# SSD decays from running sums that are spread over the partitions by DMA, in a two-layer Mamba-2 and stick-breaking trunk

## The chip, the cores and the metric

The kernel runs on one core of a Trainium2 chip. The core has TensorE (PE, matmuls; its weight loads are listed as PEld), VectorE (DVE), ScalarE (ACT), GpSimd (POOL) and SyncE (SP, which here only issues DMAs). They run side by side, each one through its own list of instructions in order, and wait for each other on semaphores. The metric is the device time of one execution in microseconds, as the median of several runs.

## The reference, cut to what matters

The input is one sequence of 512 tokens of width 1024. Layer 0 is a Mamba-2 (SSD) mixer with a squared-ReLU MLP behind it, layer 1 a stick-breaking attention with a second MLP; each of the four is followed by a LayerNorm on the scaled residual. Only the mixer's scan is touched. With 32 heads in 8 groups, a state of 128 and a time step for each head and token:

```python
dt = softplus(dt_raw + dt_bias)
a  = -exp(a_log)
da = dt * a                                   # log decay of one token, one head
a_cs = cumsum(da) within a chunk              # running sums
decay_mat = exp(segsum(da))                   # exp(a_cs[t] - a_cs[s]) for s <= t, otherwise 0
y_diag = einsum("bcgls,bcgrls,bcsgrp->bclgrp", C B^T, decay_mat, x * dt)
states = B^T (exp(a_cs[-1] - a_cs) * x * dt)  # carried from chunk to chunk
y_off  = C state * exp(a_cs)
y = rms_norm((y_diag + y_off + d * x) * silu(z)) @ w_out
```

The reference uses chunks of 64 tokens; the kernel uses chunks of 128, which gives the same sums.

## The kernel before, in words

All large products keep float32 precision by splitting both factors into a high part, rounded to the format that TensorE reads (float32r), and a low part, the rest. `mm3` (lines 206 to 209) then makes three matmuls: high by high, high by low, low by high. Weights come by DMA on SP's queue through two raw buffers; ScalarE casts the high part (line 190), and VectorE subtracts the low part (line 192), GpSimd for every fourth weight.

The mixer works on 8 groups of 4 heads, and on 4 chunks of 128 tokens, a tile having 128 partitions. For each group, `in_bc` and `in_x` project the input onto B, C and two tiles of x, `conv` applies the causal convolution and SiLU, `in_xt` turns x so that tokens lie on partitions and multiplies it by the time step, and `in_z` projects the gate. `time_steps` makes the time steps of all heads once, at the start: a projection, a transposition, softplus by elementwise work on VectorE, the log decays `da` (split into `da_h` and `da_l`), and four small matmuls with a triangle of ones and with all ones, which give the running sums and the chunks' totals. Their exponentials are `E`, `bdec` and `dec_s`.

`decays` then makes for a group and each chunk the matrix exp(a_cs[t] - a_cs[s]), with s on the partitions and, in one row, four heads by 128 tokens t. GpSimd writes `da[s]` where t >= s and 0 elsewhere (line 771, once for the high and once for the low part, into `dm`); two matmuls with a triangle (lines 774 and 775) sum it over the partitions into PSUM; ScalarE takes the exponential (line 777). `scores` makes B against C for all chunks, copies it to SBUF and lets GpSimd zero the part above the diagonal (line 788). `front` multiplies decays by scores (line 799, on GpSimd for chunk 3 and on VectorE for the others), splits the product into the factor `W` (lines 801 and 802) and updates the state. `back` multiplies `W` with x and the carried state with C. `gate` and `finish` apply the gate and the group's norm and transpose the result.

The order is a planner's, with a simulated clock: it takes the program order as priority, and issues on each engine what it thinks is ready. Program order is: the group's own `front` and `back` steps, and between them, as fillers, steps of projections of the next group and of this group's gate. After groups 3 and 7 the output projection follows. `table_order` keeps SiLU and exponential instructions of ScalarE from mixing, since they need different tables.

Of the kernel before, what the change touches and what calls it, by code (L numbers as in the profile page):

```python
# [35 lines left out]
def trunk(ctx: ExitStack, tc: tile.TileContext, io):  # L36
# [5 lines left out]
    lp = ctx.enter_context(tc.tile_pool(name="lp", bufs=2))  # L42
    ps = ctx.enter_context(tc.tile_pool(name="ps", bufs=4, space=PSUM))

    def psum(tag, shape, name):
        return ps.tile(shape, F32, tag=tag, name=name, bufs=4)
# [20 lines left out]
    for _ in range(14):  # L67
# [497 lines left out]
    def ssm(sp, nxt_ln):  # L565
# [48 lines left out]
        bdec = small("bdec")  # L614
        dec_s = small("dec_s")

        def time_steps():
            w = wdt
            pd = psum("mm", [P, T], "pdt")
            proj(pd, w, x_)  # L620
            dT = sp.tile([P, T], F32, tag="cacc", name="dT", bufs=3)
# [23 lines left out]
            nc.vector.tensor_copy(da_h, da)  # L645
            nc.vector.tensor_sub(da_l, da, f(da_h))
            pa = psum("bg", CH, "pacs")
            pt_ = psum("bg", CH, "ptot")
            for o, l in ((pa, tri_le), (pt_, ones_r)):
                nc.tensor.matmul(o, l, da_h, start=True, stop=False)  # L650
                nc.tensor.matmul(o, l, da_l, start=False, stop=True)
            nc.scalar.activation(E, pa, AF.Exp)
            nc.scalar.activation(bdec, pt_, AF.Exp)
# [107 lines left out]

        def decays(q, cs=range(NT)):
            g = q.g
            hs = slice(4 * g, 4 * g + 4)
            if cs[0] == 0:
                q.dec = []
            for c in cs:
                nm = f"{g}_{c}"
                dm = pair(f"dm{nm}", S4, "dm", 1)
                for o, i in zip(dm, (da_h, da_l)):  # L770
                    nc.gpsimd.affine_select(o, f(i[:, c, hs]).unsqueeze(2).to_broadcast(S4), pattern=[[0, 4], [1, P]],
                                            compare_op=ALU.is_ge, fill=0.0, base=0, channel_multiplier=-1)
                pseg = psum("bg", S4, f"sg{nm}")
                nc.tensor.matmul(pseg, tri_gt, dm[0], start=True, stop=False)
                nc.tensor.matmul(pseg, tri_gt, dm[1], start=False, stop=True)
                dec = sp.tile(S4, F32, tag="dec", name=f"dec{nm}", bufs=4)
                table_order("exp", nc.scalar.activation(dec, pseg, AF.Exp))
                q.dec.append(dec)

        def scores(q):  # L780
            g = q.g
            pcb = psum("bg", [P, NT, P], f"cb{g}")
            for c in range(NT):
                cs = slice(c * P, (c + 1) * P)
                mm3(pcb[:, c, :], (q.B[0][:, cs], q.B[1][:, cs]), (q.C[0][:, cs], q.C[1][:, cs]), True, True)
            q.cbm = sp.tile([P, NT, P], F32, tag="cbm", name=f"cbm{g}", bufs=1)
            nc.scalar.copy(q.cbm, pcb)
            nc.gpsimd.affine_select(q.cbm, q.cbm, pattern=[[0, NT], [1, P]], compare_op=ALU.is_ge, fill=0.0,
                                    base=0, channel_multiplier=-1)
            q.pr = [None] * NT  # L790
            q.W = [None] * NT

        def front(q, c):
# [3 lines left out]
            dec = q.dec[c]  # L797
            eng = nc.gpsimd if c == 3 else nc.vector
            eng.tensor_tensor(dec, dec, q.cbm[:, c, :].unsqueeze(1).to_broadcast(S4), op=ALU.mult)
            W = q.W[c] = pair(f"W{nm}", S4, "W", 2)  # L800
# [74 lines left out]

        cur = Group(0)
        time_steps()
        run(in_bc(cur, 0))
        run(in_bc(cur, 1))
        run(in_x(cur, 0))  # L880
        run(in_x(cur, 1))
        decays(cur)
        in_xt(cur)
        v = None
        for g in range(G):
# [15 lines left out]
            front(q, 1)  # L901
            fill.run(5)
            back(q, 0)
            fill.run(4)
            front(q, 2)
            fill.run(4)
            back(q, 1)
            fill.run(4)
            front(q, 3)
            fill.run(4)  # L910
# [21 lines left out]
            if g % 4 == 3:  # L932
# [5 lines left out]
                else:  # L938
                    nxt_ln.load_rows(lambda j, c0: sp.tile(S4, F32, tag="dec", name=f"lnr{j}{c0}", bufs=4)
                                     .rearrange("p a c -> p (a c)"), T)  # L940
# [339 lines left out]
```

## Time and profile before

| | before |
|---|---|
| median of 3 runs | 1426.51 us (1426.31 to 1427.24) |
| the profiled execution's own time | 1426.79 us |
| its span, from first to last instruction | 1424.7 us |
| mean granted TensorE clock | 0.994 |
| TensorE busy | 1394.1 us, 98% |
| VectorE, ScalarE, GpSimd busy | 1078.2, 783.9, 221.4 us |
| the mixer | the first 430 us, roughly |

A profile page lists, for each engine, its busy time; a group of instructions has its line in the kernel, its engine and operation, output and inputs by name, its shape, the count, the busy time, the mean duration in ns, and the idle time of the engine just before it with what ended that. In a timeline the first two numbers are the start and the duration in us. [...]

### The profile page before, as it was taken

Reading aid. Unit: us, or ns where it says so; the run is one execution under the profiler, and the core shown is the slowest. Engines: PE = TensorE matmul, PEld = TensorE weight load, DVE = VectorE, ACT = ScalarE, POOL = GpSimd, SP = SyncE. Lnnn points to the kernel's source line nnn. Section 1 sums busy time; section 2 is a strip of 40 time slices with the busy share of each in tenths; the row PEclk is TensorE's granted clock in tenths of the full one; section 3 lists DMA queues with packets and bytes.
Section 4 is the critical chain, followed back from the end, with each engine's and each line's share of the span. In section 5 each row is a group of like instructions: output and inputs, shape, how many; then the busy total and the mean of one; then the engine's idle time right before and its main releaser. Section 6 shows DMA issues by size and latency. Waiting matters only on the chain. (4 is left out here: it accounts for less than half of the span.)

```text
span 1424.7 us, 19323 instructions
## 1 busy us (share of the span) xinstructions
PE 1394.1 (98%) x7414; PEld 1199.9 (84%) x7414; DVE 1078.2 (76%) x1530; ACT 783.9 (55%) x1264; POOL 221.4 (16%) x249
## 2 busy tenths in 40 slices
PE   9999999999999999999999899999999999999996
PEld 6898897889997988888888789899878888888885
DVE  5798898368877695876849868787867876858587
ACT  5556574246653453626345468898842735454453
POOL 2344555135443100000000200000000000000001
PEclk9999999999999999999999999999999999999999
DMA  5223212221223356455443421121223455454533
GB/s 185 75 77 131 75 60 75 89 89 60 75 75 104 125 157 179 132 179 161 148 148 120 146 89 38 52 75 45 89 75 118 131 165 162 149 175 136 176 111 126
DMA packets 46699, 162.99 MB, mean 114 GB/s; under 512 B 5520, under 2 KB 5776, under 8 KB 46608
## 3 DMA queue, kind: packets, MB, share of 16 engines
q1 hardware_dynamic: 44016, 157.44, 35.4%
q10 hardware_dynamic: 2592, 4.33, 1.0%
q8 instruction: 58, 0.95, 0.3%
q14 instruction: 33, 0.27, 0.1%
HBM read 159.65 MB, written 2.10 MB: 114 GB/s over the span
## 5 line engine op out<-in xcount | busy, mean ns | idle before, releaser
L190 ACT CAST wh<-wr 128x1024 fp32r<-128x1024 f32 x235 | 246.7, 1050 | 328.5 <-DMA wr<-w 165.1
L192 DVE TENSOR_TENSOR wl<-wr,wh 128x1024 fp32r<-128x1024 f32 x218 | 268.4, 1232 | 184.3 <-ACT wh L190 182.9
L208 PE MATMUL f<-ln_hl,wh 128*128 128x512 f32 (+1 forms) x544 | 201.2, 371 | 0.0
L209 PE MATMUL f<-ln_hh,wl 128*128 128x512 f32 (+1 forms) x544 | 201.1, 370 | 0.0
L207 PE MATMUL f<-ln_hh,wh 128*128 128x512 f32 (+1 forms) x544 | 200.4, 371 | 0.0
L208 PEld LDWEIGHTS f<-ln_hl,wh 128*128 128x128 f32 x544 | 102.3, 188 | 17.6 <-DVE ln_hl L399 0.2
L209 PEld LDWEIGHTS f<-ln_hh,wl 128*128 128x128 f32 x544 | 102.3, 188 | 17.4
L207 PEld LDWEIGHTS f<-ln_hh,wh 128*128 128x128 f32 x544 | 101.9, 188 | 17.5
L347 POOL TENSOR_TENSOR ln_rs<-ln_sums 128x1 f32<-128x1 f32 (+1 forms) x6 | 3.1, 523 | 635.3 <-ACT lnr L345 635.3
L208 PE MATMUL X<-wl,hP 128*128 128x512 f32 x192 | 74.7, 389 | 0.0
L207 PE MATMUL X<-wh,hP 128*128 128x512 f32 x192 | 74.7, 389 | 0.0
L209 PE MATMUL X<-wh,l 128*128 128x512 f32 x192 | 74.2, 390 | 0.2 <-DVE l L460 0.2
L209 PE MATMUL pz<-wh,x_l 128*128 128x256 f32 x256 | 72.8, 284 | 0.0
L208 PE MATMUL pz<-wl,x_h 128*128 128x256 f32 x256 | 72.6, 284 | 0.0
L207 PE MATMUL pz<-wh,x_h 128*128 128x256 f32 x256 | 72.5, 283 | 0.0
L459 ACT CAST hP<-r 128x512 fp32r<-128x512 f32 x80 | 48.1, 620 | 32.4 <-DVE r L471 31.5
L192 POOL TENSOR_TENSOR wl<-wr,wh 128x1024 fp32r<-128x1024 f32 x17 | 42.5, 2503 | 93.3 <-ACT wh L190 92.9
L207 PE MATMUL px<-x_h,wh 128*128 128x512 f32 x128 | 50.8, 397 | 0.0
L208 PE MATMUL px<-x_l,wh 128*128 128x512 f32 x128 | 50.2, 393 | 0.0
L209 PE MATMUL px<-x_h,wl 128*128 128x512 f32 x128 | 50.2, 392 | 0.0
L208 PE MATMUL Y<-wl,hP 128*128 128x512 f32 x128 | 49.8, 389 | 0.0
L208 PEld LDWEIGHTS pz<-wl,x_h 128*128 128x128 f32 x256 | 48.7, 190 | 0.9
(1365 smaller groups left out, 3930.7 us busy)
## 6 DMA issues: line engine op xcount, KB each, us to landing
wr<-w SPq DMA_DIRECT2D x160, 512.0 KB, 3.6
wr<-w_bc SPq DMA_DIRECT2D x16, 512.0 KB, 3.6
wr<-w_x SPq DMA_DIRECT2D x16, 512.0 KB, 3.6
wr<-w_z SPq DMA_DIRECT2D x16, 512.0 KB, 3.5
wr<-w_so SPq DMA_DIRECT2D x16, 512.0 KB, 3.6
rawa<-w SPq DMA_DIRECT2D x16, 512.0 KB, 3.6
rawc<-w SPq DMA_DIRECT2D x16, 512.0 KB, 4.5
wr<-w_qk SPq DMA_DIRECT2D x16, 512.0 KB, 3.6
```

Source lines behind the costliest of these rows:

```text
L190: nc.scalar.copy(hi, raw)
L192: eng.tensor_sub(lo, raw, f(hi))
L207: nc.tensor.matmul(out, a[0], b[0], start=start, stop=False, skip_group_check=skip)
L208: nc.tensor.matmul(out, a[0], b[1], start=False, stop=False, skip_group_check=skip)
L209: return nc.tensor.matmul(out, a[1], b[0], start=False, stop=stop, skip_group_check=skip)
L347: nc.gpsimd.tensor_add(rs, self.sq[:, t0:t1, 0], self.sq[:, t0:t1, 1])
L459: nc.scalar.copy(h, src)
```

## The change

Four things change in the mixer.

First, the decays. One exponential of a difference is written as exp(a_cs[t] + (-a_cs[s])). `time_steps` keeps the negated running sums `ncs` with tokens on partitions, and makes the running sums a second time, laid out as rows (chunk and head on partitions, tokens along the row) by two more matmuls; a copy and a DMA put these rows into a DRAM tensor `cs_rows`. The new `spread` reads, for a group and a chunk, the four heads' rows of 128 tokens back by a DMA that repeats them on all 128 partitions, and GpSimd replaces what lies above the diagonal by -1e30 in place. `decays` then is four exponentials of 128 columns for each chunk, one for each head, in place and with `ncs` as a bias for each partition. The selects into `dm`, the two matmuls and the constant `tri_gt` go. The `dec` tiles come from 6 buffers instead of 4; the `dm` tiles' memory is free.

Second, the scores are no longer masked, since the decay is already exactly 0 above the diagonal, and `front` multiplies chunk 3 on VectorE like the others.

Third, the order. At the start, the steps of the time steps' projection alternate in program order with B's, and from the fifth on with two of C's each; the rest of `time_steps` is cut in two by a `yield`, of which the second part stands between the two x projections. `spread` for the next group follows each `front`.

Fourth, after group 3 `decays` for the next group comes behind `finish` instead of ahead of it.

```diff
+    dp = ctx.enter_context(tc.tile_pool(name="dp", bufs=1, space=bass.MemoryType.DRAM))
...
-    tri_gt = cp.tile([P, P], F32R, name="tri_gt")
-    nc.gpsimd.affine_select(tri_gt, one, pattern=[[-1, P]], compare_op=ALU.is_gt, fill=0.0,
-                            base=0, channel_multiplier=1)
...
+        ncs = small("ncs")
+        cs_rows = dp.tile([NT, H, P], F32, name="cs_rows")
...
-        def time_steps():
-            w = wdt
-            pd = psum("mm", [P, T], "pdt")
-            proj(pd, w, x_)
+        def time_steps(pd):
...
+            yield
             pa = psum("bg", CH, "pacs")
             pt_ = psum("bg", CH, "ptot")
...
+            pr = psum("mm", [P, P], "pcsr")
+            for i, x in enumerate((da_h, da_l)):
+                nc.tensor.matmul(pr, x.rearrange("p c h -> p (c h)"), tri_le, start=i == 0, stop=i == 1)
+            rows = sp.tile([P, P], F32, name="csr")
+            nc.scalar.copy(rows, pr)
+            nc.sync.dma_start(cs_rows.rearrange("c h t -> (c h) t"), rows)
+            nc.scalar.activation(ncs, pa, AF.Copy, scale=-1.0)
...
-        def decays(q, cs=range(NT)):
...
-                dm = pair(f"dm{nm}", S4, "dm", 1)
-                for o, i in zip(dm, (da_h, da_l)):
-                    nc.gpsimd.affine_select(o, f(i[:, c, hs]).unsqueeze(2).to_broadcast(S4), pattern=[[0, 4], [1, P]],
-                                            compare_op=ALU.is_ge, fill=0.0, base=0, channel_multiplier=-1)
-                pseg = psum("bg", S4, f"sg{nm}")
-                nc.tensor.matmul(pseg, tri_gt, dm[0], start=True, stop=False)
-                nc.tensor.matmul(pseg, tri_gt, dm[1], start=False, stop=True)
-                dec = sp.tile(S4, F32, tag="dec", name=f"dec{nm}", bufs=4)
-                table_order("exp", nc.scalar.activation(dec, pseg, AF.Exp))
+        def spread(q, c):
+            g = q.g
+            if c == 0:
+                q.dec = []
+            dec = sp.tile(S4, F32, tag="dec", name=f"dec{g}_{c}", bufs=6)
+            nc.sync.dma_start(dec.rearrange("p h t -> p (h t)"),
+                              cs_rows[c, 4 * g:4 * g + 4, :].rearrange("h t -> (h t)").partition_broadcast(P))
+            nc.gpsimd.affine_select(dec, dec, pattern=[[0, 4], [1, P]], compare_op=ALU.is_ge, fill=-1e30,
+                                    base=0, channel_multiplier=-1)
+            q.dec.append(dec)
+
+        def decays(q):
+            for c, dec in enumerate(q.dec):
+                for h in range(4):
+                    i = 4 * q.g + h
+                    table_order("exp", nc.scalar.activation(dec[:, h, :], dec[:, h, :], AF.Exp,
+                                                            bias=ncs[:, c, i:i + 1]))
...
-            nc.gpsimd.affine_select(q.cbm, q.cbm, pattern=[[0, NT], [1, P]], compare_op=ALU.is_ge, fill=0.0,
-                                    base=0, channel_multiplier=-1)
...
-            eng = nc.gpsimd if c == 3 else nc.vector
-            eng.tensor_tensor(dec, dec, q.cbm[:, c, :].unsqueeze(1).to_broadcast(S4), op=ALU.mult)
+            nc.vector.tensor_tensor(dec, dec, q.cbm[:, c, :].unsqueeze(1).to_broadcast(S4), op=ALU.mult)
...
-        time_steps()
-        run(in_bc(cur, 0))
-        run(in_bc(cur, 1))
+        pd = psum("mm", [P, T], "pdt")
+        b_steps, c_steps = in_bc(cur, 0), in_bc(cur, 1)
+        for k, _ in enumerate(proj_steps(pd, wdt, x_)):
+            next(b_steps)
+            if k >= KD // 2:
+                next(c_steps)
+                next(c_steps)
+        steps = time_steps(pd)
+        next(steps)
+        run(b_steps)
+        run(c_steps)
         run(in_x(cur, 0))
+        run(steps)
         run(in_x(cur, 1))
+        for c in range(NT):
+            spread(cur, c)
         decays(cur)
...
+            def first(c):
+                front(q, c)
+                if nxt:
+                    spread(nxt, c)
+
             scores(q)
             fill.run(4)
-            front(q, 0)
+            first(0)
...
-            if nxt:
+            if nxt and g % 4 < 3:
                 decays(nxt)
             finish(q, 1 if nxt else 2)
+            if nxt and g % 4 == 3:
+                decays(nxt)
```

More of the change, by code (lines that the diff above doesn't have):

```diff
@@ L896, in ssm @@
                 fill.add(in_x(nxt, 1))
+            def first(c):
+                front(q, c)
+                if nxt:
+                    spread(nxt, c)
             scores(q)
             fill.run(4)
-            front(q, 0)
+            first(0)
             fill.run(5)
-            front(q, 1)
+            first(1)
             fill.run(5)
@@ L904, in ssm @@
             fill.run(4)
-            front(q, 2)
+            first(2)
             fill.run(4)
@@ L908, in ssm @@
             fill.run(4)
-            front(q, 3)
+            first(3)
             fill.run(4)
@@ L938, in ssm @@
                 else:
-                    nxt_ln.load_rows(lambda j, c0: sp.tile(S4, F32, tag="dec", name=f"lnr{j}{c0}", bufs=4)
+                    nxt_ln.load_rows(lambda j, c0: sp.tile(S4, F32, tag="dec", name=f"lnr{j}{c0}", bufs=6)
                                      .rearrange("p a c -> p (a c)"), T)
```

5 lines of the change are left out of this document (removed).

## The prediction

> **What bounds the kernel now.** I read the page first, then a table by stretches, the waits of TensorE, and last the matmuls one by one.
>
> ```profile
> span 1424.7 us, 19323 instructions
> PE 1394.1 (98%) x7414; PEld 1199.9 (84%) x7414; DVE 1078.2 (76%) x1530; ACT 783.9 (55%) x1264; POOL 221.4 (16%) x249
> ```
> ```profile
> 62.00:215.00 153.00, 151.06 (x957) 135.70 (x957) 140.28 (x224) 96.17 (x176) 75.85 (x77) 1.00 0.25 81
> ...
> 265.00:420.00 155.00, 155.00 (x988) 140.22 (x987) 119.09 (x188) 88.42 (x153) 61.67 (x65) 1.00 0.26 79
> ```
> ```profile
> PE so L207 <- DVE v L298: 1.6, 1, 1.6
> PE pdt L208 <- DVE x_l L590: 1.4, 1, 1.4
> PE pyt L864 <- DVE yg L859: 1.4, 1, 1.4
> ```
>
> The change touches only the SSD mixer, the first 430 us. The stretch 62:215 holds groups 0 to 3, 265:420 groups 4 to 6 and the start of 7; the columns after the length are PE, PEld, DVE, ACT, POOL, clock, DMA share and GB/s. TensorE never rests: the three waits shown are the longest between 16.3 and 430 us and make 4.4 us. So a matmul taken away there is worth its place in TensorE's queue, as long as no other engine becomes the limit. The candidate is VectorE: 140.28 of 153.00 us (92%) in the first stretch, 119.09 of 155.00 (77%) in the second. ScalarE (63%) and GpSimd (50%) have room.
>
> **The matmuls that go.** Lines 774 and 775 write the segment sums, two matmuls of 512 columns for each of 4 chunks in 8 groups: eight tiles of 8, 64 matmuls. The first and the last of the eight:
>
> ```profile
> L774 PE MATMUL sg<-dm_0h,tri_gt x8: 393/476/481, 49.1 to 399.3; 128*128 128x512 f32 x8
> ...
> L775 PE MATMUL sg<-dm_3l,tri_gt x8: 389/477/485, 60.4 to 413.1; 128*128 128x512 f32 x8
> ```
>
> The 0.39 to 0.48 us in these rows is latency and overlaps the next matmul. What a matmul takes out of the queue is the distance from its start to the next start:
>
> ```profile
> 56.28 0.40 PE L774 MATMUL sg<-dm_2h,tri_gt 128*128 128x512 f32 x1
> 56.52 0.28 PE L209 MATMUL pz<-wh,x_l 128*128 128x256 f32 x1
> ...
> 57.12 0.40 PE L775 MATMUL sg<-dm_2l,tri_gt 128*128 128x512 f32 x1
> 57.35 0.28 PE L208 MATMUL pz<-wl,x_h 128*128 128x256 f32 x1
> ...
> 59.61 0.39 PE L774 MATMUL sg<-dm_3h,tri_gt 128*128 128x512 f32 x1
> 59.84 0.82 PE L727 MATMUL pxt<-ident,ca_x 128*128 128x128 f32 x6
> 60.41 0.48 PE L775 MATMUL sg<-dm_3l,tri_gt 128*128 128x512 f32 x1
> 60.73 0.38 PE L727 MATMUL pxt<-ident,ca_x 128*128 128x128 f32 x2
> ```
>
> That is 0.24, 0.23, 0.23 and 0.32 us, mean 0.255; 64 x 0.255 = 16.3 us. Two matmuls of 128 columns are added (the running sums laid out as rows). Their nearest rows are the four running-sum matmuls that exist:
>
> ```profile
> 48.39 0.22 PE L650 MATMUL pacs<-da_h,tri_le 128*128 128x128 f32 x1
> ...
> 48.79 0.40 PE L702 MATMUL pbt<-ident,ca_B 128*128 128x128 f32 x2
> ```
>
> Four in 0.40 us, so two cost 0.2 us. TensorE's gross relief is 16.3 - 0.2 = 16.1 us, 2.0 us in each group.
>
> **GpSimd.** Its selects on the decay inputs (eight groups of rows, largest and smallest shown), its select on the scores and its multiplication for chunk 3 go:
>
> ```profile
> L799 POOL TENSOR_TENSOR dec<-dec,cbm 128x512 f32<-128x512 f32 x8 | 13.0, 1626 | 0.7
> L771 POOL TENSOR_SCALAR_AFFINE_SELECT dm_2l<-da_l 128x512 fp32r<-128x512 f32 x8 | 8.7, 1088 | 1.3 <-PE sg L775 1.1
> ...
> L788 POOL TENSOR_SCALAR_AFFINE_SELECT cbm<-cbm 128x512 f32<-128x512 f32 x8 | 5.6, 695 | 32.4 <-ACT cbm L787 32.4
> L771 POOL TENSOR_SCALAR_AFFINE_SELECT dm_1l<-da_l 128x512 fp32r<-128x512 f32 x8 | 5.1, 643 | 0.1
> ```
>
> The eight groups of line 771 lie between 5.1 and 8.7 us; at the middle, 6.9, they make 55. With 5.6 and 13.0 that is 74 us. 32 selects in place on the decay tile come; line 788 is the same shape and type, so 32 x 0.695 = 22 us. GpSimd does some 52 us less in the 430 us. It is not the bound, so this is worth something only through VectorE.
>
> **VectorE.** It takes over chunk 3's multiplication, and it is the engine with the least room.
>
> ```profile
> L799 DVE TENSOR_TENSOR dec<-dec,cbm x24: 676/680/2877, 67.3 to 421.1; 128x512 f32<-128x512 f32 x24
> L802 DVE TENSOR_TENSOR W_3l<-dec,W_3h x8: 676/996/2928, 91.4 to 428.1; 128x512 fp32r<-128x512 f32 x8
> ```
> ```profile
> L799 DVE TENSOR_TENSOR dec<-dec,cbm 128x512 f32<-128x512 f32 x24 | 23.5, 1028 | 1.0 <-POOL cbm L788 1.0
> L802 DVE TENSOR_TENSOR W_3l<-dec,W_3h 128x512 fp32r<-128x512 f32 x8 | 9.6, 1201 | 0.0
> ```
>
> Eight more multiplications at the median of 0.68 us are 5.4 us, 2.7 in each half. The same rows say that such an instruction takes 0.68 us alone and up to 2.9 us at times: 24 x (1.028 - 0.680) = 8.4 us of line 799 is stretch, and 8 x (1.201 - 0.676) = 4.2 us of one of line 802's four tiles. If the stretch is GpSimd's doing, cutting 52 us of GpSimd's 138 in the two stretches (221 in the whole kernel) returns 24 to 38% of it, say 30%. Over the two lines, 8.4 us and four tiles of at most 4.2, that is 30% of at most 25 us: 7.5 us, or 3.7 in each half. Bounds: 0 (the new selects stretch as much) and 25 us. I take 3.7 against 2.7, about no net change; VectorE's 140 us then stand against a first stretch of 153 - 8 = 145 us, 97%.
>
> [...]
>
> So I credit groups 0 to 3 with 5.5 of their 8 us, since 97% can't be scheduled without new waits, and groups 4 to 7 with 7.5 of 8: 13.0 us.
>
> **ScalarE.** One exponential of 512 columns becomes four of 128 with a bias.
>
> ```profile
> L777 ACT ACTIVATE dec<-sg 128x512 f32<-128x512 f32 x32 | 19.0, 596 | 14.0 <-PE sg L775 13.9
> ```
> ```profile
> 51.16 0.26 ACT L655 COPY dtt<-pacs 128x128 f32<-128x128 f32 x1
> 51.31 0.30 ACT L653 ACTIVATE bdec<-ptot 128x128 f32<-128x128 f32 x1
> ```
>
> A piece of 128 columns costs between 0.15 us (start to start) and 0.30 us (its duration), so four cost 0.60 to 1.2 us against 0.60: 0 to 19 us more over 32 chunks, at most 2.4 in a group. I take 0 on the end: ScalarE has 57 us free in the first stretch, the waits on the segment sums (13.9 us) disappear, and TensorE meanwhile runs the next group's projections. Without that cover it would be 2.4 us a group, which would eat the gain.
>
> [...]
>
> **DMA and queues.** 32 broadcast reads of 256 KB, and one 64 KB write, join the weights on SP's queue.
>
> ```profile
> lnr<-lnrow ACTq DMA_DIRECT2D x12, 256.0 KB, 3.6
> out<-v SPq DMA_DIRECT2D x8, 256.0 KB, 2.0
> ```
> ```profile
> SPq L166 <- DVE wl L192: 63.4, 10, 8.8
> ...
> SPq L166 <- DVE xt L737: 14.0, 1, 14.0
> ```
>
> The norm's rows are the same broadcast, 3.6 us. 8.4 MB more at a DMA share of 0.25 is no load. But SP waits in order: weight transfers sat there for a buffer 6.3 us in the mean (63.4 / 10), 14.0 at worst, and a read behind one waits too. What follows it: a select on GpSimd, with the adds of lines 832 and 841 behind it, and the exponentials on ScalarE, with the weight casts behind them. Six buffers for four tiles let two reads of the next group go a whole group ahead; the last is issued some 12 filler steps (about 8 us of TensorE) before its use, against 3.6 + 0.7. I take 0; without the cover, the mean wait.
>
> **The start.** The write, the first reads and a select come between the running sums and the first product.
>
> ```profile
> 46.23 0.29 DVE L646 TENSOR_TENSOR da_l<-dtt,da_h 128x128 fp32r<-128x128 f32 x1
> ```
> ```profile
> 66.70 1.83 POOL L799 TENSOR_TENSOR dec<-dec,cbm 128x512 f32<-128x512 f32 x1
> ```
>
> From 46.5 (decays ready): 2.3 for matmuls as now (48.8), 0.3 copy, 2.0 write, 3.6 read, 0.7 select and 1.2 exponentials make 56.6 us, ten before the product at 66.7. Hidden. Interleaving the time steps' projection with B and C is already what the planner does:
>
> ```profile
> 14.11 3.91 DVE L590 TENSOR_TENSOR x_l<-xf,x_h 128x512 fp32r<-128x512 f32 x4 [2.95 <-ACT x_h L589]
> 14.23 0.39 PE L207 MATMUL pdt<-x_h,wdthi 128*128 128x512 f32 x1
> 14.46 0.40 PE L207 MATMUL pB<-x_h,wh 128*128 128x512 f32 x1
> ...
> 16.26 0.50 PE L208 MATMUL pdt<-x_l,wdthi 128*128 128x512 f32 x1 [1.40 <-DVE x_l L590]
> ```
>
> The time steps' matmuls and B's already stand mixed, and the stall is for x's low part, which the edit leaves where it is: 0, between -1.4 and +1.4. Moving group 3's exponentials behind its last transposes, the larger buffer count and the masking before the exponential instead of after the scores cost nothing I can find; the output projection between groups 3 and 4 covers the first.
>
> **Sum.** 1424.7 - 13.0 = 1411.7 us of span; the profiled execution took 1426.79, 2.1 outside it, and the median is 1426.51, so 1413.5 us.
>
> **Rivals.** (1) VectorE binds in groups 0 to 3: no stretch is returned there, its 2.7 us come on top, and the first half gives nothing; the second gives 7: 1419.5. For it: 92% now. Against: the second half's 77%, and a GpSimd with less to do. (2) Slower: the reads come too late behind waiting weight transfers, and in each group the exponentials start the mean SP wait late, 6.3 us, less some 3 us that the fillers cover: 8 x 3.3 = 26, less 16.1, is +10: 1436. It decides from 2.0 us a group, where it eats the gain. For it: SP's waits above. Against: reads a group ahead. (3) No change: the removed matmuls only filled places where TensorE would have waited for the products of lines 799 and 802; 1426.5. For it, VectorE's queue; against it, waits of only 4.4 us.
>
> **Chances.** Forecast (between 1409 and 1417) 0.62, rival 1 0.18, rival 2 0.12, rival 3 0.08. Its low end: the gross 16.1 and the start's 1.4, 1409, and 1 us more if returned stretch shortens TensorE's waits: 1408. The range goes up to no change, 1427, and leaves out rival 2 and the tails. A change under 0.2% (3 us) can't be told from none. Faster 0.79, same 0.08, slower 0.13.
>
> **What would show it.** Right: no wait of TensorE over 2 us in the mixer, its end some 13 us earlier, nothing after it changed; VectorE over 93% busy in groups 0 to 3, and line 802's mean well under 1.2 us. The exponentials' start distance tells 0.15 from 0.30. Rival 1 shows as TensorE waiting for W or conv tiles, rival 2 as GpSimd's selects waiting for a DMA. I am wrong if the mixer shortens by less than 8 us, or if groups 4 to 7 gain less than groups 0 to 3.

## The result, and the profile after

The changed kernel takes 1440.95 us in the median of 4 runs (1440.25 to 1443.22), against 1426.59 us (1426.31 to 1427.24) for four runs of the kernel before (the table ahead has the median of three, 1426.51): the ratio is 1.0104, with a 95% interval of 1.0091 to 1.0117. The change makes the kernel 14.4 us slower.

The first lines of the page after:

```profile
span 1439.4 us, 19329 instructions
...
PE 1391.4 (97%) x7352; PEld 1196.5 (83%) x7352; DVE 1062.4 (74%) x1538; ACT 804.9 (56%) x1364; POOL 174.5 (12%) x200
```

TensorE lost 62 matmuls, as the diff says (64 gone, two added), and GpSimd went from 221.4 to 174.5 us. But the span grew by 14.7 us. The stretches of the mixer after show where to look (length, then the busy time of PE, PEld, DVE, ACT and POOL with counts, then clock, DMA share and GB/s):

```profile
16.30:62.00 45.70, 33.39 (x148) 27.26 (x149) 24.23 (x45) 21.52 (x32) 3.52 (x3) 0.85 0.32 89
62.00:215.00 153.00, 149.50 (x947) 134.89 (x946) 124.95 (x210) 104.50 (x214) 51.15 (x55) 0.98 0.36 112
...
265.00:420.00 155.00, 154.52 (x949) 138.05 (x949) 109.33 (x175) 83.91 (x159) 46.24 (x45) 1.00 0.31 97
```

TensorE rests 12.3 us (45.70 - 33.39) in the first of these stretches, before the first group's scan has begun; in the kernel before it was busy for all of these 45.70 us. Its waits from 16 to 430 us after (total, times, longest):

```profile
PE pacs L648 <- DVE da_h L642: 11.0, 1, 11.0
PE pyt L866 <- DVE yg L861: 4.1, 2, 3.9
PE pbt L707 <- ACT ca_B L679: 2.9, 4, 1.0
PE st L205 <- ACT xe0h L744: 1.5, 1, 1.5
```

One wait of 11.0 us, of the running sums' matmul for the log decays, is most of it. The timeline of TensorE around it (start, duration, and in brackets the idle time before the instruction and what ended it):

```profile
33.78 0.55 PE L707 MATMUL pbt<-ident,ca_B 128*128 128x128 f32 x3 [1.04 <-ACT ca_B L679]
...
45.36 0.48 PE L648 MATMUL pacs<-da_h,tri_le 128*128 128x128 f32 x1 [11.03 <-DVE da_h L642]
...
45.85 0.41 PE L652 MATMUL pcsr<-tri_le,da_h 128*128 128x128 f32 x1
46.06 0.73 PE L205 MATMUL px<-x_h,wh 128*128 128x512 f32 x1
46.59 0.63 PE L206 MATMUL px<-x_l,wh 128*128 128x512 f32 x1
47.02 0.63 PE L207 MATMUL px<-x_h,wl 128*128 128x512 f32 x1
```

The same 11.1 us in the kernel before, and then in the kernel after together with the 4.8 us that follow:

```profile
34.30:45.40 11.10, 11.10 (x50) 9.19 (x49) 10.46 (x23) 5.42 (x8) 0.00 (x0) 1.00 0.38 121
```
```profile
34.30:45.40 11.10, 0.07 (x2) 0.04 (x1) 10.07 (x26) 5.63 (x8) 0.00 (x0) 0.61 0.29 95
45.40:50.20 4.80, 4.80 (x13) 3.93 (x14) 0.23 (x1) 0.00 (x0) 0.00 (x0) 0.50 0.00 0
```

VectorE is as busy in both, with the softplus and the log decays among its work. Before, TensorE ran 50 matmuls of x's and the next group's B and C projections meanwhile; after, only the ends of two transpositions (0.07 us) fall into these 11.1 us. Then it restarts at a granted clock of 0.50. Behind `pcsr`, the new matmul that lays the running sums out as rows, stand all projections. The reason lies in one line of the change:

```python
pr = psum("mm", [P, P], "pcsr")
```

A PSUM tile has a tag with 4 buffers here, and by the reading that fits the timelines these are handed out in program order. `mm` is the tag of all projections. In the new program order the second x projection of group 0 comes behind `pcsr`, so it and every later projection get their buffers after it, and the planner set them behind it on TensorE. `pacs` and `ptot` use the tag `bg`; they too wait for `da_h`, but before the change no projection stood behind them.

How far the kernel after lags behind the kernel before, at the same point of the work (start of the first matmul of a kind, read from both timelines, in us):

```
                                  before    after     lag
group 1's B projection             37.7      54.1    +16.4
group 0's output transposed       106.5     115.8     +9.4
first output projection           217.7     228.9    +11.3
group 3's output transposed       236.5     252.8    +16.3
first matmul behind the mixer     469.6     484.0    +14.4
```

The lag is all there at 54 us, and behind the mixer 14.4 us of it are left. The smaller lags between don't show time made good: the planner can move a group's transpositions against the projections. In e9 below, a run with the same stall that saves nothing, group 0's transpositions start at 116.4 us, a lag of 9.9 us, though the lag is 15.9 us ahead of them and at the end.

### The profile page after: what moved, and what is told of

Read it like the earlier page. It is cut to its first block, busy times and chain, and to the rows that moved or that the text cites. A ratio compares the mean times of both kernels' runs of the same rounds, so it can differ in the third digit from the quotient of the medians.

```text
span 1439.4 us, 19329 instructions
## 1 busy us (share of the span) xinstructions
PE 1391.4 (97%) x7352; PEld 1196.5 (83%) x7352; DVE 1062.4 (74%) x1538; ACT 804.9 (56%) x1364; POOL 174.5 (12%) x200
## 5 line engine op out<-in xcount | busy, mean ns | idle before, releaser
L205 PEld LDWEIGHTS pz<-wh,x_h 128*128 128x128 f32 x256 | 49.3, 193 | 0.3
```

The source lines that it names most:

```text
L205: nc.tensor.matmul(out, a[0], b[0], start=start, stop=False, skip_group_check=skip)
```

## The experiments

Each is compared with the kernel before, run again on the same chip; its medians lay between 1426.56 and 1427.32 us. Differences between two experiments are differences of their medians, some of them from different chips.

### The start: which PSUM buffers the rows take

e1_bg is the change with the row tile in the other tag.

```diff
-            pr = psum("mm", [P, P], "pcsr")
+            pr = psum("bg", [P, P], "pcsr")
```

> The changed kernel with one word changed: the PSUM tile of the running sums laid out as rows (pcsr) comes from the tag of the small products (bg) instead of the tag of the projections (mm). Theory A (buffers of one tag are handed out in program order, so the second x projection and everything in that tag behind it had to wait until the running sums' matmul could start): TensorE's wait of 11.0 us at 34 us is gone, and so is the half clock right after it (4.7 us at half speed, 2.4 us lost), and the stalls of group 0 that follow from the late start shrink (another 3 to 5 us): 1441 - 14 to 19 = 1422 to 1427 us. Theory B (the broadcast reads come late behind waiting weight transfers, in every group): only the 11 us go, GpSimd still waits some 70 us for the reads, TensorE still stalls about as much after 62 us: 1430 us or more.

Measured: 1429.38 us (1425.92 to 1435.46), ratio 1.0022 (1.0007 to 1.0037). The 11 us stall is gone and the kernel is 11.6 us faster than the change as it is. But it lies between the ranges expected, and still a little above before: the stall isn't all.

To measure the disputed line by itself, e9_before_mmrow is the kernel before with the new order of the start and the two row matmuls with their copy, and nothing that reads the rows: no DMA, bias or select, and the segment sums as before. e10_before_bgrow differs in the tag alone.

```diff
+            pr = psum("mm", [P, P], "pcsr")
+            for i, x in enumerate((da_h, da_l)):
+                nc.tensor.matmul(pr, x.rearrange("p c h -> p (c h)"), tri_le, start=i == 0, stop=i == 1)
+            rows = sp.tile([P, P], F32, tag="dec", name="csr", bufs=4)
+            nc.scalar.copy(rows, pr)
```
```diff
-            pr = psum("mm", [P, P], "pcsr")
+            pr = psum("bg", [P, P], "pcsr")
```

> The kernel before with the new order at the start and, added between the running sums and their exponentials, the two matmuls and the copy that lay the running sums out as rows; nothing reads the rows, and the decays are made as before, without any DMA read, bias or select on them. The PSUM tile has the projections' tag (mm). Theory A: the tag alone is enough: TensorE waits about 11 us for da_h at 34 us, part of it at half clock afterwards: 1426 + 10 to 15 = 1436 to 1441 us. If the broadcast reads and the exponentials are what made the changed kernel slow: 1426 to 1428 us.

> The same kernel, with the tile in the small products' tag (bg). Theory A: no wait for da_h: 1424 to 1428 us, and 10 us or more under its pair. Otherwise the two times of the pair agree.

Measured: e9 1442.46 us (1440.90 to 1442.55), ratio 1.0107 (1.0090 to 1.0124); e10 1427.10 us (1424.33 to 1428.79), ratio 1.0001 (0.9991 to 1.0010). The longest waits of TensorE in e9, and in e10:

```profile
PE pacs L648 <- DVE da_h L642: 11.0, 1, 11.0
PE so L207 <- DVE v L298: 3.1, 1, 3.1
```
```profile
PE so L207 <- DVE v L298: 2.1, 1, 2.1
PE pdt L208 <- DVE x_l L590: 1.2, 1, 1.2
```

The same work in another buffer makes 15.4 us, and the 11.0 us wait is there in one and not in the other. e9's lag on before is 15.9 us at group 1's B projection and 15.9 us at the first matmul behind the mixer: it loses this once and gains nothing back. In e10 TensorE has no gap where the changed kernel stands still:

```profile
34.30:45.40 11.10, 11.10 (x52) 9.17 (x51) 10.60 (x22) 9.04 (x13) 0.00 (x0) 1.00 0.44 142
```

The two runs differ in the tag alone, so the tag is the cause of the slowdown; that it acts through the order in which buffers are handed out is the reading that fits the timelines. Two other parts of the change were tried for it. e3_startonly is the kernel before with the new order of the start alone:

```diff
+        pd = psum("mm", [P, T], "pdt")
+        b_steps, c_steps = in_bc(cur, 0), in_bc(cur, 1)
+        for k, _ in enumerate(proj_steps(pd, wdt, x_)):
+            next(b_steps)
...
         run(in_x(cur, 0))
+        run(steps)
         run(in_x(cur, 1))
```

> The kernel before with only the new order at the start: the time steps' projection interleaved with B and C, and the running sums between the two x projections; decays as before, so no rows tile, no DMA, no biased exponentials. Theory A: the running sums use the small products' tag, so nothing waits for them, and the time is that of the kernel before, 1426.5 us within 2. If the interleaving itself or the place of the running sums is the cause: 1436 us or more, with TensorE waiting for da_h.

Measured: 1425.71 us (1424.33 to 1426.70), ratio 0.9990 (0.9980 to 0.9999). The order alone does no harm; it hurts only together with a tile that joins the projections' tag. e2_oldfin is the change with the old place of `decays` after group 3, and e4_bg_oldfin is that together with e1's edit:

```diff
-            if nxt and g % 4 < 3:
+            if nxt:
                 decays(nxt)
...
-            if nxt and g % 4 == 3:
-                decays(nxt)
```

> The changed kernel with only the order at the end of group 3 as before: the exponentials of group 4 ahead of group 3's norm. Theory A: the stall of 11 us at the start stays, the 4.0 us wait of the transposes at 253 us and the half clock behind it (10.2 us at half speed) may go: 1441 - 0 to 9 = 1432 to 1441 us. Theory B: no change, 1441 us. If the moved exponentials were the main cause, it would come down to 1427 us or less.

> Both edits of the two runs ahead (pcsr in the small products' tag, exponentials of group 4 ahead of group 3's norm). Theory A: the sum of what the two give alone: 1413 to 1425 us, and below the kernel before. Theory B: 1428 us or more, since the reads are as late as in the changed kernel.

Measured: e2 1441.36 us (1438.98 to 1444.14), ratio 1.0107 (1.0082 to 1.0132), beside 1440.95 for the change; e4 1430.23 us (1427.49 to 1431.67), ratio 1.0027 (1.0018 to 1.0036), beside 1429.38 for e1. Where `decays` is called there makes no difference that can be told.

### Why the change without its stall is still not faster

What were the 64 matmuls worth? e13_nosg is the kernel before without them: the exponential reads the masked decays straight, so the sums over the chunk are left out. e14_split is the kernel before, complete, with each exponential cut into the four biased ones of the change (the bias is zero); e16_nosg_split is both.

```diff
-                pseg = psum("bg", S4, f"sg{nm}")
-                nc.tensor.matmul(pseg, tri_gt, dm[0], start=True, stop=False)
-                nc.tensor.matmul(pseg, tri_gt, dm[1], start=False, stop=True)
...
-                table_order("exp", nc.scalar.activation(dec, pseg, AF.Exp))
+                table_order("exp", nc.scalar.activation(dec, f(dm[0]), AF.Exp))
```
```diff
-                table_order("exp", nc.scalar.activation(dec, pseg, AF.Exp))
+                for h in range(4):
+                    table_order("exp", nc.scalar.activation(dec[:, h, :], pseg[:, h, :], AF.Exp, bias=zb))
```

> The kernel before without the 64 segment-sum matmuls; the exponential is taken straight from the masked decays (so the sums over the chunk are left out), everything else is as before. Theory F (the forecast's term was right, 64 x 0.255 = 16.3 us, and the changed kernel loses it again to its new work): 1426.6 - 13 to 16 = 1411 to 1414 us. Theory G (with less to do, TensorE runs out of fillers and waits at the ends of the groups, so the term itself is smaller): 1417 to 1423 us, with waits of pyt, po or st of 1 to 4 us in groups 0 to 3 or at the mixer's end, and stretches of half clock.

> The kernel before with each exponential of 512 columns cut into four of 128 with a bias from memory (a column of zeros, so the values are the same). It prices the exponentials alone. By the start distance that the changed kernel shows, 0.294 us, four take 1.18 us instead of 0.5 us: 2.7 us more on ScalarE in each group. If TensorE's work covers that: 1425 to 1428 us. If it stands on the chain that closes each group: 1431 us or more.

> The run without the segment-sum matmuls (the sums over the chunk left out again), with the exponentials in four pieces with a bias. If the pieces are what gives the relief back: 5 us or more above the run without the matmuls. If they are covered: within 2 us of it.

Measured: e13 1422.35 us (1421.92 to 1423.35), ratio 0.9964 (0.9951 to 0.9977); e14 1432.90 us (1430.69 to 1433.46), ratio 1.0032 (1.0018 to 1.0046); e16 1422.42 us (1421.99 to 1423.35), ratio 0.9966 (0.9953 to 0.9979). Without the matmuls the kernel gains 5.0 us (1427.32 - 1422.35), not 16. The cut exponentials cost 5.6 us with the segment sums in place, and nothing without them. The first half in e13, and its longest waits of TensorE:

```profile
62.00:215.00 153.00, 144.74 (x899) 128.05 (x898) 133.70 (x209) 91.29 (x164) 80.67 (x81) 1.00 0.25 83
```
```profile
PE pyt L861 <- DVE yg L856: 2.8, 2, 1.7
PE st L207 <- ACT xe2h L739: 1.6, 1, 1.6
...
PE py L834 <- DVE pv L809: 1.4, 1, 1.4
```

Stretches cut at fixed times hold different work in two kernels. So here is the whole mixer, from 16.3 us to the first matmul behind it, before and in e13:

```profile
16.30:469.59 453.29, 446.77 (x2653) 393.63 (x2653) 358.01 (x564) 244.98 (x426) 186.10 (x188) 1.00 0.27 83
```
```profile
16.30:465.21 448.91, 434.95 (x2589) 383.02 (x2589) 356.70 (x564) 245.11 (x425) 186.02 (x188) 1.00 0.27 84
```

TensorE rests 6.5 us of it before (453.29 - 446.77) and 14.0 us in e13: 7.5 us of the 16.3 turn into rest, and the mixer ends 4.4 us earlier. The other 4.4 us show as no rest; the matmuls that stay start that much further apart in all. TensorE now waits at many small places, for the group's norm (`yg`), the state's input (`xe`), the carried state (`pv`). VectorE's capacity doesn't look like the reason, with 133.70 of 153 us busy in the first half against 140.28 before. The reading is that these chains were as long before, with matmuls to cover them; no run shows a chain by itself.

### The end of group 3, and ScalarE's order

In the change all 16 exponentials of a group are ready early, since they no longer wait for TensorE. In e1 they stand ahead of the last copy of group 3's output, `yl`, on ScalarE. Timelines of e1, ScalarE's, then TensorE's:

```profile
221.81 1.28 ACT L782 ACT_TABLE_LOAD   x1
223.11 1.57 ACT L782 ACTIVATE dec<-dec,ncs 128x128 f32<-128x128 f32 x5
224.99 2.44 ACT L782 ACTIVATE dec<-dec,ncs 128x128 f32<-128x128 f32 x8
...
227.74 0.97 ACT L782 ACTIVATE dec<-dec,ncs 128x128 f32<-128x128 f32 x3
228.61 0.34 ACT L842 COPY yl<-py 128x256 f32<-128x256 f32 x1
```
```profile
237.81 0.69 PE L866 MATMUL pyt<-ident,yg 128*128 128x128 f32 x2 [3.63 <-DVE yg L861]
```

e5_gatefirst is e1 with the exponentials ordered behind the group's four squares of the gate on ScalarE (an order, no wait):

```diff
+        squares = []
...
-                    table_order("exp", nc.scalar.activation(dec[:, h, :], dec[:, h, :], AF.Exp,
-                                                            bias=ncs[:, c, i:i + 1]))
+                    ins = nc.scalar.activation(dec[:, h, :], dec[:, h, :], AF.Exp, bias=ncs[:, c, i:i + 1])
+                    table_order("exp", ins)
+                    for other in squares:
+                        tc.add_manual_dep(ins.ins, other.ins.name,
+                                          mybir.DependencyInfo(mybir.DependencyClass.NoSync,
+                                                               mybir.DependencyReason.DATA), reason="gate first")
...
-            nc.scalar.activation(q.sz[c // 2][:, c % 2, :], yc, AF.Square, accum_out=q.ss[:, c:c + 1])
+            squares[c:] = [nc.scalar.activation(q.sz[c // 2][:, c % 2, :], yc, AF.Square, accum_out=q.ss[:, c:c + 1])]
```

e6_wide is e1 with the bias added by GpSimd and one exponential of 512 columns for each chunk; e8_wide_gf has both edits.

```diff
+            nc.gpsimd.tensor_tensor(dec, dec, ncs[:, c, 4 * g:4 * g + 4].unsqueeze(2).to_broadcast(S4), op=ALU.add)
...
-                for h in range(4):
...
+                table_order("exp", nc.scalar.activation(dec, dec, AF.Exp))
```

> The running sums' rows in the small products' tag, and on ScalarE the exponentials of the next group ordered behind the four squares that end this group's gate. Theory C (sixteen biased exponentials, 0.294 us apart, all ready at once since they no longer wait for TensorE, stand on ScalarE ahead of the last copies of this group's result, and TensorE then waits for that result at the end of group 3): the transposes of group 3 start about 6 us earlier than the 237.8 us with the tag alone, TensorE's wait of 3.6 us there and the 10.2 us at half clock around it are gone: 1429.4 - 7 to 12 = 1417 to 1422 us. Theory B (late reads): no gain, 1428 to 1431 us.

> The running sums' rows in the small products' tag; the bias is added by GpSimd (one addition of 512 columns ahead of the select), and ScalarE takes one exponential of 512 columns for each chunk instead of four of 128. Theory C: the block on ScalarE shrinks from 16 x 0.294 = 4.7 us to 4 x 0.5 = 2.0 us a group, so about half of the gain of the ordering: 1429.4 - 2 to 6 = 1423 to 1427 us. Against it: 32 additions of some 1.4 us on GpSimd, which stretch VectorE. If that weighs more, 1430 us or above. Theory B: the same time as with the tag alone, within 1.5 us.

> All three: the tag, the exponentials behind the squares, and one exponential of 512 columns with the bias added by GpSimd. Theory C: the block is already off the closing chain of the group by the ordering, so the short block helps only the start of the next group: within 3 us of the ordering with biased exponentials, 1415 to 1424 us.

Measured: e5 1422.70 us (1420.26 to 1423.20), ratio 0.9967 (0.9954 to 0.9980); e6 1430.76 us (1428.55 to 1433.73), ratio 1.0030 (1.0021 to 1.0039); e8 1425.91 us (1423.06 to 1428.74), ratio 0.9997 (0.9987 to 1.0007). The order is worth 6.7 us (1429.38 - 1422.70; single runs of e1 spread over 9.5 us). In e5 `yl` comes first, and the transposes follow without a wait (ScalarE, then TensorE):

```profile
223.81 0.37 ACT L848 COPY yl<-py 128x256 f32<-128x256 f32 x1 [1.98 <-POOL yg L849]
...
228.23 3.04 ACT L784 ACTIVATE dec<-dec,ncs 128x128 f32<-128x128 f32 x10
```
```profile
229.28 1.04 PE L872 MATMUL pyt<-ident,yg 128*128 128x128 f32 x8
```

The same 11 us in e1 and in e5:

```profile
236.00:247.00 11.00, 8.63 (x31) 7.56 (x32) 8.59 (x18) 4.86 (x9) 1.36 (x2) 0.54 0.27 89
```
```profile
236.00:247.00 11.00, 10.40 (x53) 8.69 (x52) 10.14 (x14) 4.61 (x7) 2.77 (x1) 1.00 0.46 144
```

Besides the wait of 3.6 us, e1 loses time by a granted clock of 0.54 in this stretch. Fewer instructions on ScalarE (e6) gained nothing, and lost 3.2 us beside e5 when the order was there (e8). e6 also puts 32 additions on GpSimd, so it doesn't tell whether shorter exponentials alone would help.

### The reads

e7_actq is e1 with the broadcast reads on ScalarE's DMA queue, which carries little else. e11_gf_actq is e5 with the same edit, and e12_gf_actq_oldstart is e11 with the start in the old order, the time steps first.

```diff
-            nc.sync.dma_start(dec.rearrange("p h t -> p (h t)"),
+            nc.scalar.dma_start(dec.rearrange("p h t -> p (h t)"),
```
```diff
-        b_steps, c_steps = in_bc(cur, 0), in_bc(cur, 1)
...
+        proj(pd, wdt, x_)
+        run(time_steps(pd))
+        run(in_bc(cur, 0))
+        run(in_bc(cur, 1))
```

> The running sums' rows in the small products' tag; the 32 broadcast reads are issued on ScalarE's DMA queue instead of SP's, so they stand behind no weight transfer. Theory B: GpSimd's wait for the reads (42 us over 27 reads with the tag alone) falls under 15 us, and the time by 5 us or more, to 1424 us or less. Theory C: GpSimd's waits may fall, but the time stays at 1427 to 1432 us, since the exponentials stand in the same block; ScalarE pays 32 issues of some 0.35 us.

> The tag, the exponentials ordered behind the squares, and the broadcast reads on ScalarE's DMA queue. If the two gains over the tag alone (6.7 us for the order, 6.5 for the queue) are two causes: 1414 to 1418 us. If both only happened to shift the planner's order, they don't add: 1420 to 1425 us.

> The same with the start as in the kernel before: the time steps first in program order, then B, C and x. The start alone changed the kernel before by -0.9 us, so within 3 us of the run ahead: if that gives 1416, 1413 to 1419 us. If the running sums, and with them the rows, come some 3 us earlier and this counts, a little lower.

Measured: e7 1422.90 us (1421.59 to 1426.32), ratio 0.9975 (0.9966 to 0.9985); e11 1422.11 us (1420.46 to 1423.55), ratio 0.9966 (0.9953 to 0.9979); e12 1429.03 us (1424.59 to 1430.56), ratio 1.0011 (1.0000 to 1.0022). e7 gains 6.5 us on e1, but not by shorter waits for the reads. GpSimd's wait for them in e1, and the same with TensorE's longest in e7:

```profile
POOL dec L774 <- DMA dec<-cs_rows: 42.2, 27, 7.6
```
```profile
POOL dec L774 <- DMA dec<-cs_rows: 43.1, 23, 7.7
...
PE pyt L866 <- DVE yg L861: 6.7, 1, 6.7
```

Nor is it e5's gain by another way, since the wait at group 3's end grew to 6.7 us. The gain is in the groups ahead of it: TensorE is busy 151.27 of the 153 us from 62 to 215 us in e7, 147.98 in e1. Yet the two gains don't add (e11 and e5 can't be told apart). With another queue the planner writes out another order; what in it gains 6.5 us stays open. So does e12: 6.9 us slower than e11, without a stall at the start. It loses time around group 3's end, where TensorE rests 5.0 us from 215 to 265 us, and none in e11.

Whether reads among the weights on SP's queue cost anything was measured by itself, in the kernel before, with 28 reads that nobody uses: in e15_reads256 reads of 1 KB to 128 partitions into one spare tile, in e17_reads_dec reads of the change's size, 256 KB, into the decay tiles behind their last use.

```diff
+        def bread():
+            x = sp.tile([P, 256], F32, tag="br", name="br", bufs=1)
+            nc.sync.dma_start(x, io["lnrow"][0, 0, :256].partition_broadcast(P))
```
```diff
+        def bread(q, c):
+            nc.sync.dma_start(q.dec[c].rearrange("p h t -> p (h t)"), io["lnrow"][0, 0, :T].partition_broadcast(P))
```

> The kernel before with four broadcast reads more in each of 7 groups on SP's queue, one behind each front, 1 KB for each of 128 partitions (half the size of the changed kernel's, for want of memory), from an input, into one buffer that nothing reads. It prices the reads' place in SP's queue alone. If weights run far enough ahead: 1425 to 1428 us. If the queue matters: 1430 us or more.

> The kernel before with 28 broadcast reads of 256 KB more on SP's queue, each into a decay tile behind its last use, so each waits for its W_l as the changed kernel's reads do and none can run ahead as in the run of small reads. Nothing reads what they bring. If the reads' place in SP's queue costs by itself: 1430 us or more, with weights landing late and TensorE waiting for wh or wl. If not, and the 29 us of the small reads came only from 76 us of SP's queue blocked in the first 100 us: 1425 to 1428 us.

Measured: e15 1455.79 us (1454.07 to 1456.39), ratio 1.0196 (1.0181 to 1.0211); e17 1427.85 us (1426.22 to 1429.35), ratio 1.0003 (0.9993 to 1.0013). e15 didn't test what it was for, as SP's waits and its 28 issues (shortest, median and longest in ns, first and last start) show:

```profile
SPq L782 <- DMA br<-lnrow: 75.9, 27, 6.0
```
```profile
L782 SPq DMA_DIRECT2D br<-lnrow x28: 327/328/432, 8.1 to 100.5; - x28
```

The reads depended on nothing, so they were all issued in the first 100 us instead of one behind each `front`. Each waited in SP's queue for the one before, 2.8 us on average, and the weights stood behind them. e17's reads wait for real work:

```profile
dec<-lnrow SPq DMA_DIRECT2D x28, 256.0 KB, 3.7
```

They land in 3.7 us, and the kernel's time doesn't change.

### The best version

e18_gf_actq_pool3 is e11 with chunk 3's multiplication back on GpSimd.

```diff
-            nc.vector.tensor_tensor(dec, dec, q.cbm[:, c, :].unsqueeze(1).to_broadcast(S4), op=ALU.mult)
+            eng = nc.gpsimd if c == 3 else nc.vector
+            eng.tensor_tensor(dec, dec, q.cbm[:, c, :].unsqueeze(1).to_broadcast(S4), op=ALU.mult)
```

> The tag, the order behind the squares, the reads on ScalarE's queue, and the multiplication of chunk 3 on GpSimd again as in the kernel before. If VectorE were what holds the mended kernel at 1422 us: 2 us or more below that, 1420 us or less. If VectorE isn't the limit (it is busy 126 of 153 us in the stretch 62:215 with the first three edits): 1421 to 1425 us.

Measured: 1421.55 us (1418.64 to 1423.35), ratio 0.9958 (0.9942 to 0.9974), beside e11's 0.9966 (0.9953 to 0.9979): no difference between the two that can be told. VectorE isn't the limit without its help, as e11's first half shows:

```profile
62.00:215.00 153.00, 145.24 (x910) 129.50 (x910) 126.28 (x214) 104.39 (x217) 59.32 (x60) 1.00 0.38 116
```

With its two faults mended, the change is worth 4 to 6 us: e5, e11 and e18 all beat both kernels, by about as much as removing the matmuls alone does (e13). That gain hangs on the planner's order as a whole: e12 has both faults mended too, only the start in the old order, and gains nothing (1429.03 us).

## Why the prediction was wrong

It forecast 1413.5 us, and no rival's time, nor the range, held 1440.95.

**The step that failed: "The start … Hidden".** The prediction followed the chain of data, from the decays at 46.5 us through write, read and select to the product at 66.7, and found ten us of room. It put the start at 0, between -1.4 and +1.4 us. It never asked which buffer the new row tile takes and what stands behind that. The sum takes for granted that TensorE goes on with the projections while the decays are made, and the change put the projections behind those decays. e9 against e10 gives the price: 15.4 us. The chain itself was later than forecast too. SP's issues after:

```profile
54.47 0.33 SPq L655 DMA_DIRECT2D cs_rows<-csr  x1
56.02 3.49 SPq L772 DMA_DIRECT2D dec<-cs_rows  x6
```

The first reads were issued at 56.0 us, instead of at 51.1 by the prediction's steps (46.5 + 2.3 + 0.3 + 2.0). That alone did no harm: the first product starts at 64.0 us (line 801 below), not later than the 66.7 us before.

**The second: the main term of the sum, "16.1 us".** Count and price were right (64 matmuls gone; all 64 distances in the trace of before add up to 16.2 us), but their sum was taken as the gain, less a discount for VectorE: 13.0 us. Leaving the matmuls out gained 5.0 us (e13), and TensorE rested 7.5 us more. "TensorE never rests" was read as "a matmul taken away there is worth its place in TensorE's queue". The short waits before said only that the chains beside the matmuls were covered by them. Rival 3 had this idea ("the removed matmuls only filled places where TensorE would have waited") and got a chance of 0.08. Of the 11.3 us that weren't gained it is right for 7.5 at least, but it named the products of lines 799 and 802 as what TensorE would wait for, and e13's longest waits are for others.

**VectorE at "97%" of the first stretch: wrong.** Lines 801 and 804 after, the multiplications and one of the subtractions (shortest, median and longest in ns):

```profile
L801 DVE TENSOR_TENSOR dec<-dec,cbm x32: 672/685/1154, 64.0 to 437.2; 128x512 f32<-128x512 f32 x32
L804 DVE TENSOR_TENSOR W_3l<-dec,W_3h x8: 679/992/1415, 97.3 to 444.3; 128x512 fp32r<-128x512 f32 x8
```

VectorE was busy 124.95 of the 153 us, 82%, and 126.28 in e11, with no stall to thin it out. Over the whole kernel it has eight instructions more and is busy 15.8 us less (1078.2 to 1062.4). The multiplications' mean fell from 1.028 to 0.699 us and their longest from 2877 to 1154 ns, so nearly all their stretch is gone together with GpSimd's work, where 30% was taken. The subtraction's longest fell from 2928 to 1415 ns, but its median stayed (996 before, 992 after), and its mean went from 1.201 only to 0.988 us (1.203 in e1), so not every instruction gained. Rival 1 is excluded: VectorE wasn't the bound.

**ScalarE, "0 on the end": wrong in place, not in price.** Of the two prices set out, 0.15 and 0.30 us for a piece, the upper one holds:

```profile
62.68 4.80 ACT L782 ACTIVATE dec<-dec,ncs 128x128 f32<-128x128 f32 x16
```

Fifteen distances and one duration of 0.39 us (the mean of a piece) make 4.80, so a piece starts 0.294 us after the one before. ScalarE had room enough for that (104.50 of 153 us busy from 62 to 215 us), but at group 3's end the 16 pieces stand in front of the copy that closes the group; e5 shows 6.7 us for their order. In the old kernel the pieces cost 5.6 us (e14), but not in each group: group 5's transpositions start no later than before (370.6 us, 372.2 before), group 7's 6.8 us later (441.6 and 434.8). Which chain they lengthen there isn't shown.

**Right:** the reads cost nothing in SP's queue (e17, 1.0003), though GpSimd waited for them; the interleaving alone costs nothing (e3, 0.9990); nor does the place of group 3's exponentials (e2, e4). Rival 2 forecast 1436, nearest to the time of all, which was luck: it had the exponentials of each group start late behind the reads. GpSimd's selects do wait for the reads after, longest for the first one, behind the stall. But ScalarE stands idle only 0.1 us in all ahead of the exponentials (the last number of the second line), and VectorE 5.6 us for their results, 4.7 of these in the first group:

```profile
POOL dec L774 <- DMA dec<-cs_rows: 72.8, 24, 25.8
```
```profile
L782 ACT ACTIVATE dec<-dec,ncs 128x128 f32<-128x128 f32 x128 | 39.4, 388 | 0.1
```

And e5 and e11 are faster than e1, though GpSimd waits longer for the reads in them (62.6 and 69.6 us against 42.2).

**The account.** Matmuls away -5.0 (e13), row tile in the projections' tag +11.6 (change against e1), exponentials in front of group 3's end +6.7 (e1 against e5): +13.3, against 14.4 measured. The last two are steps of one chain of runs, so the sum tests only that the change without its two faults (e5, -3.9) comes near the kernel without the matmuls (e13, -5.0). With e9 against e10 for the tag, 15.4, the sum is 17.1. The 1 to 3 us between these sums and the measured time stay unexplained.

**Signs.** The prediction's first sign, no wait of TensorE over 2 us in the mixer, failed twice (11.0 and 3.9 us), and these two waits are the two faults. The mixer was to end some 13 us earlier; it ended 14.4 us later.

## What to carry to other kernels

For a new tile, ask not only when its data are ready but whose buffers it takes: here a small tile in a busy tag put everything that took a buffer after it behind its own wait (11.0 us, and 15.4 us in all: e9 against e10). A matmul removed from a TensorE that hardly waits may be worth much less than its time, here 5.0 of 16.3 us; leave the work out in one run, and see about what there is to gain, before the replacement is built. When work stops waiting for an engine it is ready early, and can then stand in front of what closes a stage: fix its order behind that.

## What the runs showed of the hardware

The granted clock fell to half without one long wait. In the changed kernel two waits of 1.5 and 1.0 us (`st` and `pbt` above, at 79.1 and 81.1 us) are followed by this:

```profile
78.00:80.00 2.00, 0.89 (x6) 0.78 (x6) 2.00 (x5) 1.48 (x2) 0.64 (x1) 1.00 0.88 295
80.00:82.00 2.00, 0.97 (x5) 0.89 (x5) 2.00 (x4) 1.83 (x4) 1.96 (x1) 0.79 0.14 57
82.00:84.00 2.00, 2.00 (x12) 2.00 (x11) 2.00 (x5) 0.99 (x2) 0.28 (x1) 0.50 0.80 246
...
86.00:88.00 2.00, 2.00 (x8) 1.61 (x7) 2.00 (x5) 1.08 (x2) 0.00 (x0) 0.50 0.42 131
88.00:90.00 2.00, 2.00 (x10) 1.67 (x9) 0.70 (x3) 0.51 (x2) 0.69 (x2) 1.00 0.44 121
```

TensorE was about half busy for 4 us, and from about 81.2 us ran at 0.50 until about 88 us, some 6.8 us, though it was busy all that time. In the clock records of the kernels before and after there are seven stretches at 0.50 that the kernel's end doesn't cut: three of 3.41 us, two of 6.83 (one of them here), one of 10.24 and one of 13.65. The longest began at 36.8 us, inside the 11.0 us wait, and ended at 50.5 us. At half clock a matmul of 512 columns held TensorE for 0.43 us (46.59 to 47.02 above); in the kernel before, at a clock of 1.00, for 0.23 (57.12 to 57.35, in the prediction's rows). There, waits of 1.0 and 1.6 us that lay 6.3 us apart (`st` to 240.10 us, `so` from 246.41 to 248.01) left the clock of their stretch at 1.00:

```profile
215.00:265.00 50.00, 47.40 (x225) 39.10 (x225) 30.93 (x41) 19.36 (x31) 19.26 (x18) 1.00 0.23 72
```

In e13 TensorE rests 8.3 us of the first half in scattered waits, also at 1.00. The two waits of the changed kernel lay 1.0 us apart (to 79.11 us, from 80.09) and made 2.5 us; the 6.83 us at half clock behind them cost another 3.4 us by estimate (6.83 x 0.50). What brought the clock down no run shows by itself; no wait before the fall, since the one of 11.0 us, was longer than 1.55 us.
